# Half of x's turns by VectorE in 32x32 blocks through DRAM, and one product with every engine in written order

## The chip, the cores and the metric

The kernel runs on one core of a Trainium2 chip. A core has a matrix engine (TensorE, PE in the profile), an engine for elementwise work and reductions (VectorE, DVE), an engine for activations, scaled copies and casts (ScalarE, ACT), a general engine (GpSimd, POOL) and an engine that here only starts loads and stores (SyncE, SP). Each takes its instructions in order, and they meet through semaphores. Loads and stores are started from SP's or POOL's queue and carried by 16 DMA engines. SBUF is the on-chip memory with 128 partitions; PSUM holds TensorE's results.

The metric is device time in microseconds (us), median of three runs. Before the change it is 787.09 us (786.91 to 787.52).

## The reference

One layer on x of 512 tokens by 2048 columns, in float32: sliding-window attention with grouped heads, then a gated embedding, then a norm.

```python
hn = rmsnorm(x, norm_g)
y = swa_mixer(hn, ...)              # projections, attention, then (out * silu(gate)) @ w_out
x = x + y
emb = p @ ple_proj
g = sigmoid(rmsnorm(x, ple_norm) @ ple_gate)
x = x + emb * g
return rmsnorm(x, final_g)
```

Two products with 2048x2048 weights follow one another: the output projection (`w_out`) and the gate (`ple_gate`). The second needs the sum x + y with its columns on the partitions, that is transposed ("turned"), and scaled by `ple_norm`. The change is in how, and when, that turning is done.

## The kernel before

A float32 product is made of three matmuls on operands split in two parts: high part by high part, high by low and low by high (`mm3`, the lines that the profile shows as L126 to L128; of 512 columns each). High parts come from a ScalarE cast (`bhi` for weights, `fh...` for the other operand), low parts from a VectorE subtraction of the cast from the original (`blo`, `fl...`).

**Blocks.** Each of the two big products is computed with seven block products in place of eight; one of the seven is itself done the same way with smaller blocks (the `small` names). The six big ones are taken in the order 1, 7, 6, 5, 3, 4. A product is two units (jj = 0, 1) of four steps (m = 0 to 3). A step is one piece of weights (128x1024, 512 KB) and 12 matmuls; after it may come half of a small product, with a piece of its own and 6 matmuls. The product that the change is about is the last of the output projection, p = 4: units (4,0) and (4,1), followed by the first product of the gate, units (1,0) and (1,1).

**One step in written order** (`unit`, L997): fetch the piece (`B.get`); the 12 matmuls; `some_later`, which takes a share of a list of additions to x that earlier products left; `todo`, the step's own chores; `between`, which prepares an operand of a small product and multiplies half a small product. Fetching piece i also issues the cast and the subtraction (the "split", L760 and L761) of piece i + 2. Three buffers hold the casts, so the cast of piece i + 2 waits until TensorE is done with piece i - 1.

**x.** It lies in SBUF as four column groups of 512 (j = 0 to 3), each with four token blocks of 128 (t). A result of a product is added to a block of it by VectorE (`add_to_x`, L1054 and L1056). When a block's last addition is made, ScalarE squares it and sums the squares along the row (`squares`, L1024), in the very next call.

**Turns.** `turn(kp, th)` (L1028) takes two column chunks of 128 (2kp and 2kp + 1) of a half of the tokens (th: blocks 2th and 2th + 1): four 128x128 transposes by TensorE into one PSUM bank (L1038), then two scaled copies of 128x256 by ScalarE into `hT` (L1041). There are 16 such calls, 64 transposes. Twelve are spread over the eight steps of p = 4, those of columns 1024 to 2047 (kp 4 to 7) first; four (kp 0 to 3, second half of the tokens) follow in the four steps of the gate's unit (1,0). `ple_forms.steps(1)` makes the first gate operand, in four parts, from the first half of the tokens of columns 1024 to 2047.

**Who orders the work.** TensorE and SP run in written order throughout. VectorE, ScalarE and GpSimd are in written order in the attention part and from the gate's second product on. In the output projection and in the gate's first product, a planner orders these three, by its own costs: it takes what it holds to be ready, and so moves instructions ahead of earlier-written ones. The load of `final_g` (`fg`, 1 MB on the SP queue) is issued after product 3.

Of the kernel before, what the change touches and what calls it, by code (L numbers as in the profile page):

```python
# [11 lines left out]
F32 = mybir.dt.float32  # L12
# [6 lines left out]
D = 2048  # L19
S = 512  # L20
P = 128
# [34 lines left out]
def trunk_kernel(ctx: ExitStack, tc: tile.TileContext, a: dict):  # L56
    nc = tc.nc
# [12 lines left out]
    pn = const.tile([P, KC], F32, name="pn")  # L70
# [8 lines left out]
    def quarter(name):  # L79
        return whole.tile([P, 4, S], F32, tag="quarter", name=name)  # L80
# [5 lines left out]
    WE = 1024  # L86
# [71 lines left out]
    def run(gen):  # L158
        for _ in gen:
            pass  # L160
# [38 lines left out]
    for k in range(KC):  # L199
# [7 lines left out]
        both = start_pool.tile([P, 2 * 768], F32R, tag="w0s", name=f"w0s{k}")  # L207
# [46 lines left out]
        else:  # L254
            high()
            if k == 1:
                src = xw[:, w_at[512] : w_at[512] + 256]
# [9 lines left out]
        f, e = k == 0, k == KC - 1  # L267
# [18 lines left out]
        for part in "hl" if f else "lh":  # L286
            for t in range(NB):
                c = slice(t * P, (t + 1) * P)
# [6 lines left out]
        if 3 <= k < 3 + NB:  # L295
            t = k - 3
# [18 lines left out]
    def evac_q(c, ps, to=None):  # L315
# [11 lines left out]
        def split(low):  # L327
# [15 lines left out]
            engines={getattr(mybir.EngineType, v) for v in ("PE", "SP", "DVE", "Activation", "Pool")}  # L343
# [57 lines left out]
    for b in range(exact, BUCKETS):  # L401
        d = np.nonzero(bk == b)[0]
        if len(d):
            lo, n = P - 1 + int(d.min()), len(d)
# [301 lines left out]
    for nm, p in SUMS:  # L706
        for q in (6, 5) if (nm, p) == ("ple_gate", 5) else (p,):
            sum_small(nm, q)
        for jj in range(2):
            for m in range(4):  # L710
                t = summed[nm, p, jj, m] = tc.dram_tile([P, WE], F32, name=f"{nm}_{p}_{jj}_{m}")
# [194 lines left out]
    blocks = TWOS * UNITS  # L906
# [83 lines left out]
    later = []  # L990
# [37 lines left out]
    def turn(kp, th, tag):  # L1028
# [10 lines left out]
        for n in range(2):  # L1039
            k = 2 * kp + n  # L1040
            nc.scalar.mul(hT[g][:, k % 4, th * 256 : th * 256 + 256], tp[:, n * 256 : n * 256 + 256], pn[:, k : k + 1])  # L1041

    ple_forms = Forms(swapped, "g")
    ple_first = ple_forms.steps(1)

# [261 lines left out]
    x_at = {(1, 0, 3): 2, (1, 1, 1): 1, (7, 0, 0): 3}  # L1307
    waiting = {(7, 0): (1, 0), (6, 0): (1, 1)}
    held = {}
    for n, p in enumerate(ORDER_OUT):  # L1310
        nxt = out_forms.steps(ORDER_OUT[n + 1]) if n < 5 else iter(())
        for jj in range(2):
            later.extend(held.pop(waiting.get((p, jj)), ()))
            calls = iter(range(4))

            def between(m, ps):
                if (p, jj, m) in EMBED_AT:
                    embedding.slot()
                q = small_steps.get((p, jj, m))
                if q is not None:  # L1320
                    small_out.prepare(q)
                for q in SMALL["w_out"].get((p, jj), {}).get(m, ()):
                    small_out.product(q)

            def todo():
                step = next(calls)
                part = x_at.get((p, jj, step))
                if part is not None:
                    load_x(part, nc.sync)
                part = embed_steps.get((p, jj, step))  # L1330
                if part is not None:
                    embedding.prepare(part)
                next(nxt, None)
                if p == 4:

                    for _ in range({0: 1, 1: 2, 2: 2, 3: 2, 5: 1, 6: 2, 7: 2}.get(4 * jj + step, 0)):
                        turn(*turns.pop(0), "o")
                    if jj:
                        next(ple_first, None)

            ps = unit(p, jj, at_out, out_forms, todo, between)
            posts = [partial_of(add_y, p, jj, tb, ps[tb]) for tb in range(2)]
            if p == 1:
                held[p, jj] = posts
            else:
                later.extend(posts)
        run(nxt)
        if p == 3:
            fg = late.tile([P, D], F32, tag="fg", name="fg")
            nc.sync.dma_start(fg, a["final_g"].partition_broadcast(P))  # L1350
        if p == 3:
            turns = [(kp, th) for kp0, th in ((4, 1), (4, 0), (0, 0)) for kp in range(kp0, kp0 + 4)]
    run(ple_first)
    assert not turns


# [141 lines left out]
    for n, p in enumerate(ORDER_PLE[:-1]):  # L1498
        if n == 1:

            ctx.enter_context(
                tc.manual_schedule(
                    engines={getattr(mybir.EngineType, v) for v in ("PE", "SP", "DVE", "Activation", "Pool")}
                )
            )
        nxt = ple_forms.steps(ORDER_PLE[n + 1])
        for jj in range(2):
            calls = iter(range(4))

            def todo():  # L1510
                step = next(calls)
                k = early.get((p, jj, step))
                if (p, jj, step) in embed_loads:
                    load_embeds(*embed_loads[p, jj, step])
                while small_due:
                    small_due.pop(0)()
                if (p, jj, step) == (5, 0, 2):
                    assert len(moves) == 4
                    while moves:
                        moves.pop(0)()  # L1520
                if (p, jj, step) == (5, 0, 3):
                    for square in moved.pop(0):
                        square()
                if turns:
                    turn(*turns.pop(0), "t")
                    if not turns:
                        nc.vector.tensor_reduce(ss2, ssq2, axis=AX.X, op=ALU.add)
                        run(power_of_mean(rstd2, ss2, "r2"))
                        nc.scalar.activation(ss2[:, :1], ss2[:, :1], AF.Sigmoid)
                    return  # L1530
                next(nxt, None)
                if p == 1:
                    next(nxt, None)
                if k is not None:
                    split_last(k)
                if (p, jj, step) in opens:
                    open_bank(*opens[p, jj, step])

            def between(m, ps):
                if (p, m) == (7, 3):  # L1540
                    gate(p, jj, ps, None)
                q = ple_steps.get((p, jj, m))
                if q is not None:
                    small_ple.prepare(q)
                for q in SMALL["ple_gate"].get((p, jj), {}).get(m, ()):
                    small_ple.product(q)
                if (p, jj, m) == (6, 1, 1):
                    later.append(partial_of(gate_later, "sum", 0, None, embeds_for(1, 0)))

            ps = unit(p, jj, at_ple, ple_forms, todo, between)  # L1550
            last_two, held_e = (p, jj) == (3, 1), {}
            if not (p == 7 or last_two):
                later.insert(0, partial_of(gate_later, p, jj, ps, held_e))
            for of, which in EMBEDS.get((p, jj), ()):
                e = embeds_for(of, which)
                held_e.update(e)
                if of == 1:
                    later.insert(1, partial_of(gate_later, "sum", which, None, dict(e)))
                    held_e.clear()
            if p == 5:  # L1560
                while moved:
                    later.extend(moved.pop(0))
        run(nxt)
# [171 lines left out]
```

## Time and profile before

| | |
|---|---|
| time, median of 3 runs | 787.09 us (786.91 to 787.52) |
| the profiled execution's own time | 787.18 us |
| its span, first to last instruction | 785.5 us |
| mean granted TensorE clock | 0.996 |
| busy: TensorE / VectorE / ScalarE / GpSimd | 775.9 / 612.1 / 528.9 / 149.7 us |
| product p = 4 of the output projection | 587.9 to 624.8 us of the span |
| the gate's unit (1,0) | 624.8 to 637.6 us |

The span is what the profiler saw between the first and the last instruction; the execution's own time holds 1.7 us more around it. Busy times are not additive: the engines work side by side. In a row of the timeline the columns are start, duration, engine, line, operation, output from inputs, shapes and count, and in brackets the idle time of that engine just before, with what ended it. Names of tiles are those of the program without their numbers.

### The profile page before, as it was taken

The numbers are of one execution on the slowest core, as the hardware profiler recorded it, in microseconds if no ns is written. First come the engines' busy times: TensorE is split into PE (matmuls) and PEld (weight loads), VectorE is DVE, ScalarE is ACT, GpSimd is POOL, SyncE is SP. The second block draws the span as 40 slices with busy tenths as digits, with TensorE's granted clock in tenths as the row PEclk, the third lists the DMA queues.
The fourth block names the chain that finished last, engine by engine and source line by source line (L and its number), as shares of the span: only waits on it lengthen the run. The fifth ranks groups of instructions, "written<-read, shape, count | busy, mean of one in ns | idle before, by whom it ended". The sixth has DMA issues, their size and how long they took to land.

```text
span 785.5 us, 11181 instructions
## 1 busy us (share of the span) xinstructions
PE 775.9 (99%) x3700; PEld 648.8 (83%) x3700; DVE 612.1 (78%) x1057; ACT 528.9 (67%) x1121; POOL 149.7 (19%) x273
## 2 busy tenths in 40 slices
PE   9999999999999999999999999999999999999995
PEld 7888888888888888888888888888888888888885
DVE  4547697877877688877878899976897958998996
ACT  6743586766767676766666655678778976667874
POOL 0201423122222314132322200001000002221111
PEclk9999999999999999999999999999999999999998
DMA  9988989999999989999997489868698179999956
GB/s 341 297 210 295 190 251 311 309 287 262 277 265 266 273 235 297 252 302 251 294 252 207 141 318 324 281 204 292 238 374 297 58 298 280 276 280 310 301 116 214
DMA packets 50393, 206.72 MB, mean 263 GB/s; under 512 B 7504, under 2 KB 8528, under 8 KB 44576
## 3 DMA queue, kind: packets, MB, share of 16 engines
q1 hardware_dynamic: 39152, 154.58, 54.9%
q0 software_dynamic: 11184, 51.44, 32.3%
q8 instruction: 29, 0.48, 0.3%
q14 instruction: 28, 0.23, 0.1%
HBM read 192.31 MB, written 75.55 MB: 341 GB/s over the span
## 4 chain that ended last, share of the span: by engine, by line
PE 97%; issue 1%; DMA 0%; DVE 0%; POOL 0%; POOLq 0%; ACT 0%; DVEq 0%; SPq 0%
PE gps L126 7%; PE gps L127 7%; PE gps L128 7%; PE qps L126 7%; PE qps L128 7%; PE qps L127 7%; PE o L127 6%; PE o L128 6%; PE o L126 6%; PE g L128 5%; PE g L127 5%; PE g L126 5%; PE s L485 2%; PE vps L290 2%; PE o L603 2%; PE pt L551 2%
## 5 line engine op out<-in xcount | busy, mean ns | idle before, releaser
L761 DVE TENSOR_TENSOR blo<-braw,bhi 128x1024 fp32r<-128x1024 f32 x100 | 121.9, 1222 | 30.7 <-ACT bhi L760 29.8
L760 ACT CAST bhi<-braw 128x1024 fp32r<-128x1024 f32 x100 | 105.0, 1050 | 39.1 <-PE o L128 15.1
L126 PE MATMUL gps<-xh,whi 128*128 128x512 f32 x256 | 100.0, 390 | 0.0
L127 PE MATMUL gps<-xl,whi 128*128 128x512 f32 x256 | 100.0, 390 | 0.0
L128 PE MATMUL gps<-xh,wlo 128*128 128x512 f32 x256 | 99.8, 390 | 0.0
L126 PE MATMUL qps<-xh,whi 128*128 128x512 f32 x224 | 87.8, 392 | 0.0
L128 PE MATMUL qps<-xh,wlo 128*128 128x512 f32 x224 | 87.5, 390 | 0.0
L127 PE MATMUL qps<-xl,whi 128*128 128x512 f32 x224 | 87.4, 390 | 0.0
L575 POOL TENSOR_SCALAR_AFFINE_SELECT own<-r 64x512 fp32r<-64x512 f32 (+1 forms) x48 | 32.4, 675 | 238.9 <-DVE r L565 235.7
L110 DVE TENSOR_TENSOR wlo<-wraw,whi 128x1024 fp32r<-128x1024 f32 x60 | 73.5, 1227 | 3.4 <-ACT whi L109 3.3
L127 PE MATMUL o<-blo,fho 128*128 128x512 f32 x192 | 74.8, 390 | 0.0
L126 PE MATMUL o<-bhi,fho 128*128 128x512 f32 x192 | 74.8, 390 | 0.0
L128 PE MATMUL o<-bhi,flo 128*128 128x512 f32 x192 | 74.8, 389 | 0.0
L109 ACT CAST whi<-wraw 128x1024 fp32r<-128x1024 f32 x60 | 62.3, 1040 | 5.2 <-issue 4.1
L126 PE MATMUL g<-bhi,fhg 128*128 128x512 f32 x160 | 62.7, 392 | 0.0
L128 PE MATMUL g<-bhi,flg 128*128 128x512 f32 x160 | 62.3, 389 | 0.0
L127 PE MATMUL g<-blo,fhg 128*128 128x512 f32 x160 | 62.3, 389 | 0.0
L128 PEld LDWEIGHTS gps<-xh,wlo 128*128 128x128 f32 x256 | 48.1, 188 | 10.3
L126 PEld LDWEIGHTS gps<-xh,whi 128*128 128x128 f32 x256 | 48.1, 188 | 9.2
L529 ACT ACTIVATE t<-t,sm 128x129 f32<-128x129 f32 (+1 forms) x128 | 49.6, 389 | 8.7 <-DVE sm L525 7.4
L127 PEld LDWEIGHTS gps<-xl,whi 128*128 128x128 f32 x256 | 48.1, 188 | 8.9
L564 ACT CAST r<-pt 128x256 fp32r<-128x256 f32 x56 | 20.8, 372 | 49.9 <-PE pt L551 49.4
(291 smaller groups left out, 1813.2 us busy)
## 6 DMA issues: line engine op xcount, KB each, us to landing
wraw<-in_w_gate_in SPq DMA_DIRECT2D x32, 512.0 KB, 7.7
w_out<-in_w_out POOLq DMA_DIRECT2D x32, 512.0 KB, 9.0
braw<-w_out SPq DMA_DIRECT2D x32, 512.0 KB, 5.4
wraw<-in_w_q SPq DMA_DIRECT2D x28, 512.0 KB, 6.5
braw<-in_w_out SPq DMA_DIRECT2D x22, 512.0 KB, 4.8
braw<-in_ple_gate SPq DMA_DIRECT2D x22, 512.0 KB, 5.8
xw<-in_first SPq DMA_DIRECT2D x14, 640.5 KB, 7.0
w_out<-in_w_out SPq DMA_DIRECT2D x16, 512.0 KB, 10.8
```

The lines of the kernel that those rows point to most:

```text
L109: nc.scalar.copy(hi, raw)
L110: nc.vector.tensor_sub(lo, raw, hi.bitcast(F32))
L126: nc.tensor.matmul(ps, sh, mh, start=first, stop=False, skip_group_check=more)
L127: nc.tensor.matmul(ps, sh, ml, start=False, stop=False, skip_group_check=more)
L128: nc.tensor.matmul(ps, sl, mh, start=False, stop=last, skip_group_check=more)
L290: nc.tensor.matmul(v_ps[t], h[:, c], part_of(high_at, 256, 512), start=f, stop=e, skip_group_check=True)
L485: nc.tensor.matmul(s_ps[:, u, : 2 * n], st, of_keys[:, first * 2 * QB : (first * QB + n) * 2], start=True, stop=True)
L529: nc.scalar.activation(su, su, AF.Exp, bias=sm[:, u : u + 1], accum_out=sm[:, 2 + u : 3 + u])
L564: nc.scalar.copy(rh, src)
L575: nc.gpsimd.affine_select(out=flat(own), in_=flat(r).bitcast(F32), pattern=[[0, 8], [sign, HB]], compare_op=ALU.is_ge, fill=0.0, base=-HB ...
L760: nc.scalar.copy(hi[:, :n], raw)
L761: nc.vector.tensor_sub(lo[:, :n], raw, hi[:, :n].bitcast(F32))
```

## The change

- **Half of the turns leave TensorE.** Columns 1024 to 2047 (j = 2 and 3), both halves of the tokens, are turned in three stages. `turn_blocks`: two VectorE transposes of 128x512, each of which turns every 32x32 block in its place, into a tile of 128x1024, and a 512 KB write of it to DRAM from POOL's queue. `gather_blocks`: four loads of 128 KB from POOL's queue, which bring the blocks of one column chunk together on 32 partitions each, in rows of 1 KB. `scale_turned`: four ScalarE copies of 128x256, scaled by `ple_norm`, from the gathered tile into `hT`. Each stage is there four times (j = 2, 3; th = 0, 1). The tiles written to DRAM come from two buffers in turn, so the third `turn_blocks` waits for the first write to have landed and the fourth for the second.
- **The stages are spread by a table**, `turns_at`: block turns in the four steps of (4,0), gathers from (4,0,2) to (4,1,1), scalings in (4,1,1), (4,1,2), (1,0,1) and (1,0,3).
- **The turns that are left** on TensorE: kp 0 to 3, first half of the tokens, two in each of the last two steps of (4,1); the four of the second half stay where they were. The parts of the first gate operand follow each of those four turns.
- **Product p = 4 is in written order on all engines**, no longer the planner's.
- **Two smaller things.** The two additions that product (3,1) leaves are taken together, at the head of the list, so that both are made in step (4,0,0). The load of `fg` moves from the end of product 3 to step (4,1,1).

```diff
--- before.py
+++ after.py
@@ -1040,6 +1040,48 @@
             k = 2 * kp + n
             nc.scalar.mul(hT[g][:, k % 4, th * 256 : th * 256 + 256], tp[:, n * 256 : n * 256 + 256], pn[:, k : k + 1])
 
+    SQ = P // 4
+    apart, gathered = {}, {}
+
+    def turn_blocks(j, th):
+
+        t = late.tile([P, WE], F32, tag="e", name=f"blocks{j}_{th}", bufs=2)
+        to = t.rearrange("p (a k t q) -> p t k a q", a=4, k=4, t=2)
+        for tb in range(2):
+            assert not missing[j, 2 * th + tb]
+            src = x1[j][:, 2 * th + tb, :].rearrange("p (k a q) -> p k a q", k=4, a=4)
+            nc.vector.transpose(to[:, tb], src)
+        apart[j, th] = tc.dram_tile([P, WE], F32, name=f"apart{j}_{th}")
+        nc.gpsimd.dma_start(apart[j, th], t)
+
+    def gather_blocks(j, th):
+
+        src = apart[j, th].rearrange("(b i) (a x) -> a i b x", b=4, a=4)
+        to = gathered[j, th] = (s7 if th else s1)[:, j % 2].rearrange("p n c -> p (n c)")
+        for quad in range(4):
+            nc.gpsimd.dma_start(to[SQ * quad : SQ * quad + SQ].rearrange("p (b x) -> p b x", b=4), src[quad])
+
+    def scale_turned(j, th):
+
+        if j not in hT:
+            hT[j] = swapped[(j + 2) % 4] = quarter(f"hT{j}")
+        src = gathered[j, th].rearrange("p (b k t q) -> p k b t q", b=4, k=4, t=2)
+        for n in range(4):
+            to = hT[j][:, n, th * 256 : th * 256 + 256].rearrange("p (t b q) -> p b t q", t=2, b=4)
+            nc.scalar.mul(to, src[:, n], pn[:, 4 * j + n : 4 * j + n + 1])
+
+    turns_at = {
+        (4, 0, 0): [(turn_blocks, 2, 0)], (4, 0, 1): [(turn_blocks, 3, 0)],
+        (4, 0, 2): [(gather_blocks, 2, 0), (turn_blocks, 2, 1)], (4, 0, 3): [(gather_blocks, 3, 0), (turn_blocks, 3, 1)],
+        (4, 1, 0): [(gather_blocks, 2, 1)], (4, 1, 1): [(scale_turned, 2, 0), (gather_blocks, 3, 1)],
+        (4, 1, 2): [(scale_turned, 3, 0)],
+        (1, 0, 1): [(scale_turned, 2, 1)], (1, 0, 3): [(scale_turned, 3, 1)],
+    }
+
+    def turns_due(at):
+        for part, j, th in turns_at.get(at, ()):
+            part(j, th)
+
     ple_forms = Forms(swapped, "g")
     ple_first = ple_forms.steps(1)
 
@@ -1307,7 +1349,15 @@
     x_at = {(1, 0, 3): 2, (1, 1, 1): 1, (7, 0, 0): 3}
     waiting = {(7, 0): (1, 0), (6, 0): (1, 1)}
     held = {}
+    fg = None
+    last_out = ExitStack()
     for n, p in enumerate(ORDER_OUT):
+        if p == 4:
+            last_out.enter_context(
+                tc.manual_schedule(
+                    engines={getattr(mybir.EngineType, v) for v in ("PE", "SP", "DVE", "Activation", "Pool")}
+                )
+            )
         nxt = out_forms.steps(ORDER_OUT[n + 1]) if n < 5 else iter(())
         for jj in range(2):
             later.extend(held.pop(waiting.get((p, jj)), ()))
@@ -1323,6 +1373,7 @@
                     small_out.product(q)
 
             def todo():
+                nonlocal fg
                 step = next(calls)
                 part = x_at.get((p, jj, step))
                 if part is not None:
@@ -1332,25 +1383,28 @@
                     embedding.prepare(part)
                 next(nxt, None)
                 if p == 4:
-
-                    for _ in range({0: 1, 1: 2, 2: 2, 3: 2, 5: 1, 6: 2, 7: 2}.get(4 * jj + step, 0)):
+                    turns_due((p, jj, step))
+                if (p, jj, step) == (4, 1, 1):
+                    fg = late.tile([P, D], F32, tag="fg", name="fg")
+                    nc.sync.dma_start(fg, a["final_g"].partition_broadcast(P))
+                if (p, jj) == (4, 1):
+                    for _ in range(2 if step >= 2 else 0):
                         turn(*turns.pop(0), "o")
-                    if jj:
                         next(ple_first, None)
 
             ps = unit(p, jj, at_out, out_forms, todo, between)
             posts = [partial_of(add_y, p, jj, tb, ps[tb]) for tb in range(2)]
             if p == 1:
                 held[p, jj] = posts
+            elif (p, jj) == (3, 1):
+                later.insert(0, lambda both=posts: [post() for post in both])
             else:
                 later.extend(posts)
         run(nxt)
         if p == 3:
-            fg = late.tile([P, D], F32, tag="fg", name="fg")
-            nc.sync.dma_start(fg, a["final_g"].partition_broadcast(P))
-        if p == 3:
-            turns = [(kp, th) for kp0, th in ((4, 1), (4, 0), (0, 0)) for kp in range(kp0, kp0 + 4)]
+            turns = [(kp, 0) for kp in range(4)]
     run(ple_first)
+    last_out.close()
     assert not turns
 
 
@@ -1521,6 +1575,8 @@
                 if (p, jj, step) == (5, 0, 3):
                     for square in moved.pop(0):
                         square()
+                if p == 1:
+                    turns_due((p, jj, step))
                 if turns:
                     turn(*turns.pop(0), "t")
                     if not turns:
```

## The prediction

> **What bounds the kernel now.** I read the page's busy line and the shares of the chain that ended last, then the chain itself around the change, then the timeline of three engines there.
>
> ```profile
> span 785.5 us, 11181 instructions
> PE 775.9 (99%) x3700; PEld 648.8 (83%) x3700; DVE 612.1 (78%) x1057; ACT 528.9 (67%) x1121; POOL 149.7 (19%) x273
> PE 97%; issue 1%; DMA 0%; DVE 0%; POOL 0%; POOLq 0%; ACT 0%; DVEq 0%; SPq 0%
> ```
>
> TensorE sets the end: whatever is taken off it is won, and whatever makes it wait is lost one for one. The profiled execution took 787.18 us, span and 1.7 us around it, against a median of 787.09, so sums on the span carry over less 0.1.
>
> The chain in order of time, from p = 4 into the gate:
>
> ```profile
> 590.80 0.44 PE tp L1038 x4
> 595.37 0.87 PE tp L1038 x8
> 600.37 0.87 PE tp L1038 x8
> 605.35 0.88 PE tp L1038 x8
> 613.26 0.39 PE o L127
> 615.95 0.44 PE tp L1038 x4
> ```
>
> A turn (four transposes) costs TensorE 0.44 us; all lie on the chain. The one other entry, at 613.26, is a matmul whose low part came late; p = 4 has no other stall. The busy times by stretch, the time before p = 4, then (4,0), (4,1) and about (1,0):
>
> ```profile
> core 0: us, PE busy (x) PEld busy (x) DVE busy (x) ACT busy (x) POOL busy (x), PEclk, DMA share, GB/s
> 566.00:587.90 21.90, 21.90 (x98) 18.14 (x97) 19.82 (x24) 16.16 (x22) 0.00 (x0) 1.00 0.96 370
> 587.90:607.50 19.60, 19.60 (x102) 16.45 (x101) 14.76 (x17) 16.21 (x32) 0.00 (x0) 1.00 0.83 305
> 607.50:624.80 17.30, 17.30 (x88) 14.21 (x86) 15.69 (x18) 15.99 (x31) 0.00 (x0) 1.00 0.15 54
> 624.80:641.00 16.20, 16.20 (x82) 13.43 (x80) 8.86 (x12) 13.72 (x27) 1.05 (x1) 1.00 0.63 231
> ```
>
> In p = 4 VectorE and ScalarE have some 10 to 25% to spare, and the planner fits their work to that. GpSimd is idle and the DMA engines nearly so in (4,1).
>
> **What is removed.** Eight turns leave p = 4 (12 become 4): 8 x 0.44 = 3.5 us off TensorE. The 16 ScalarE copies that go with them are replaced by 16 of the same size.
>
> **Units for the walk.** TensorE, then ScalarE, then VectorE, in the timeline of before:
>
> ```profile
> 592.47 0.40 PE L126 MATMUL o<-bhi,fho 128*128 128x512 f32 x1
> ...
> 595.21 1.03 PE L1038 MATMUL tp<-ident,x1s 128*128 128x128 f32 x8
> ...
> 610.15 0.39 PE L126 MATMUL smallo<-bhi,small_aho 128*128 128x512 f32 x1
> ...
> 612.87 0.39 PE L126 MATMUL o<-bhi,fho 128*128 128x512 f32 x1
> 613.15 0.50 PE L127 MATMUL o<-blo,fho 128*128 128x512 f32 x1
> 613.49 0.39 PE L128 MATMUL o<-bhi,flo 128*128 128x512 f32 x1
> ```
>
> ```profile
> 590.88 1.05 ACT L760 CAST bhi<-braw 128x1024 fp32r<-128x1024 f32 x1 [0.17 <-ACT s L1024]
> 595.45 1.05 ACT L760 CAST bhi<-braw 128x1024 fp32r<-128x1024 f32 x1 [0.90 <-ACT s L1024]
> 596.40 1.56 ACT L1041 ACTIVATE hT<-tp,pn 128x256 f32<-128x256 f32 x4
> 602.80 1.06 ACT L760 CAST bhi<-braw 128x1024 fp32r<-128x1024 f32 x1
> 603.74 0.65 ACT L1024 ACTIVATE s<-x1s 128x512 f32<-128x512 f32 x1
> 604.36 0.64 ACT L865 ACTIVATE fhg<-hT 128x512 fp32r<-128x512 f32 x1
> ```
>
> ```profile
> 588.13 1.23 DVE L761 TENSOR_TENSOR blo<-braw,bhi 128x1024 fp32r<-128x1024 f32 x1
> 589.28 0.68 DVE L1054 TENSOR_TENSOR x1s<-o,x1s 128x512 f32<-128x512 f32 x1
> 589.88 1.21 DVE L761 TENSOR_TENSOR blo<-braw,bhi 128x1024 fp32r<-128x1024 f32 x1
> 591.96 1.23 DVE L761 TENSOR_TENSOR blo<-braw,bhi 128x1024 fp32r<-128x1024 f32 x1 [0.27 <-ACT bhi L760]
> 610.74 1.23 DVE L858 TENSOR_TENSOR hT<-hT 128x1024 f32<-128x1024 f32 x1
> 611.88 2.35 DVE L761 TENSOR_TENSOR blo<-braw,bhi 128x1024 fp32r<-128x1024 f32 x2
> ```
>
> A step takes TensorE 2.72 us (592.47 to 595.21), half a small product 1.36 (two from 610.15 to 612.87). A cast can start 0.24 after TensorE has passed to the next piece (595.21, 595.45) and frees ScalarE 0.95 later (596.40). The subtraction starts 1.08 after its cast (590.88, 591.96), and VectorE is free 1.14 later (two in 2.35). An addition takes VectorE 0.60 (589.28 to 589.88), a square ScalarE 0.63 with its read-out (603.74 to 604.36). Four scaled copies took 1.56, of which 0.1 is a tail that overlaps the next (1.05 against 0.95 for a cast): 0.37 each. A form of an operand takes ScalarE 0.52 and VectorE 0.60, as other operations of 512 elements.
>
> So a split of piece i + 2, asked for when piece i starts, is done 0.24 + 1.08 + 1.14 + 0.1 = 2.56 us later. TensorE wants it after pieces i and i + 1, its low part 0.23 after that: 4.08 + 0.23 where a step and a small half lie between (1.75 us to spare), 2.72 + 0.23 where two small halves do (0.39). The stall at 613 stands just behind such a pair: pitches of 0.28 and 0.34 us where 0.227 (2.72/12) is usual, 0.16 in all.
>
> **What is added, bounded.** The block transposes occur in no row before. Below: 0.55 us, 512 elements at the pace that the 1024-element subtraction adds over a 512-element operation (1.22 - 0.68). Above: 1.22, as if it went over its data twice. I take 0.62, nearest to the 512-element rows: eight are 5.0 us of VectorE. [...]
>
> The writes and gathers ride on an idle POOL queue:
>
> ```profile
> 560.68 0.53 POOL L1245 DMA_DIRECT2D embeds<-made  x1 [3.80 <-ACT made L1256]
> embeds<-made POOLq DMA_DIRECT2D x8, 512.0 KB, 4.3
> DMA to landing us min/median/max: 2.9/5.3/11.3
> 628.88 1.05 POOL L1366 TENSOR_TENSOR rstd<-ms_r,power 128x4 f32<-128x4 f32 x1 [67.67 <-DVE ms_r L1364]
> ```
>
> A write of the same shape and queue lands in 4.3 us (by the view of the tile, its loads back included, 2.9 to 11.3). The first block write leaves at about 593, so the third block turn, which needs its buffer and whose turn on VectorE comes near 601, finds it landed up to 8 us; at 11.3 it is 3.3 us late, with two subtractions queued behind it. The gathers are 128 KB each; with 0.55 us per issue the first four land near 606, and the first scaling is due near 616: hidden unless they take 15 us. In (4,1) the DMA share is 0.15, so they and the `fg` load, which leaves the busy stretch before, meet little. POOL's own next work is at 628.88, after the last gather (issued by 615). On SP `fg` passes loads that wait for buffers anyway: nothing.
>
> **What written order costs.** Here the change is not free. In written order a step gives ScalarE: cast, then the square of the block that VectorE has just added to; and VectorE: subtraction, then that addition. The square waits for the addition, the addition stands behind the subtraction, the subtraction behind the cast. ScalarE is not free after 0.95 but after 1.08 + 1.14 + 0.60 + 0.1 + 0.63 = 3.55 us, and the next cast is queued behind. The planner could let the square wait its turn: at 602.80 it put a cast ahead of the square that starts at 603.74. I walk through the queues piece by piece:
>
> (4,0): VectorE has 8 subtractions (9.1), 4 additions (2.4), 8 block transposes (5.0) and three operations for the small operands (1.8), which the planner had partly done before 588: 18.3 us, against 4 x 4.08 = 16.3 of TensorE. It also starts 1.3 late, at 589.2, behind its first cast. 18.3 + 1.3 - 16.3 - 1.75 to spare: a stall of 1.5 us.
>
> (4,1), second step: v0 starts near 605.1; VectorE, behind by the above, ends the addition to x at 610.3, the square ends at 611.0, the cast 612.0, the subtraction 613.25; TensorE wants it at 611.2 + 0.23. Stall 1.9; with VectorE on time it would still be 0.4, since two small halves leave only 0.39.
>
> First gate operand: from the second step of (4,1), time 0: cast, subtraction, addition and square end at 3.8; four scalings 5.3; two casts 7.2; the next subtraction, addition and square end near 9.8 (the wait again); four scalings 11.3; the first turn's two copies 12.0, its form 12.6 and low part 13.3. TensorE reaches the gate at 2.72 + 1.36 + 2.72 + 0.88 + 2.72 + 0.88 = 11.3 and wants the low part 0.45 later. Stall 1.7.
>
> (1,0): the third piece's cast stands behind the rest of the forms and a square that waits; in strict order it is 2.7 late, but this product is still the planner's, which may put that cast into ScalarE's gap (0). I take 0.7, nearer to the planner, since before it moved work for the gate's second product far ahead (L858 at 610.74, for a product that starts after (1,1)).
>
> **Sum:** -3.5 + 1.5 + 1.9 + 1.7 + 0.7 - 0.2 (0.16: the stall at 613 is counted in them) = +2.1: 787.1 + 2.1 = **789.2 us**.
>
> **Rivals.** I call 0.2% (1.6 us) what a measurement can tell from no change.
>
> Faster, 783.6 to 785.3: VectorE keeps up with TensorE in (4,0), so that a step's addition is done soon after its square comes up on ScalarE, and the casts behind are not late. It decides if the squares wait less than about 0.8 us, by which a wait of 3.55 exceeds a step's 2.72. For it: TensorE had no stall with VectorE at 19.8 of 21.9 us just before, and both queues are emptier at 588 by what the planner had pulled forward. Then (4,0) costs nothing, the second step 0.4 and the gate's operand up to 1.3: -3.5 + 0 to 1.7. Against: the wait inside a step comes from the order, not from a backlog. Chance 0.28.
>
> No change, 785.5 to 788.7: two of the three stalls come, 1.9 to 3.6 us in place of 5.8. Chance 0.17.
>
> Forecast, 787.5 to 791.5: chance 0.40.
>
> Much slower, 791 to 793, in three ways. ScalarE's third cast in (1,0) stands behind the forms, 2.0 more than the 0.7 above, 791.2; it decides if the planner's part can't go ahead of the written one (0.07). Or block transposes take 1.22 us: eight times 0.6 more on VectorE, of which (4,0) passes on 3.9 by the same walk, 793.1 (0.05). Or a block write lands in over 8 us: up to +3.3, 792.5 (0.03). [...]
>
> That the turns don't leave TensorE is not to be feared: its matmuls are in written order.
>
> **How the numbers follow.** Faster 0.28. Same takes 0.17 and the low quarter of the forecast's 0.40: 0.26. Slower is the rest, 0.46. The range, 784.0 to 792.5, takes in the better part of the faster case and the usual bounds of the slower; the forecast's own is 787.5 to 791.5.
>
> **What would show it.** Right: the row of `tp` has 32 matmuls, not 64; of the two rows of waits between 585 and 690 below, the first grows to 3 us or more, and the second, 1.1 us in all, comes to 2 us for each square of (4,1); the gate's first matmuls wait for `flg`; (1,0) starts near 627, not 624.8. Wrong: (1,0) starts by 622 with no such wait; then the queues had more room than I walked. Block transposes of over 1 us, or VectorE waiting for a write to DRAM, would make it worse than the sum.
>
> ```profile
> PEld o L127 <- DVE blo L761: 0.3, 1, 0.3
> ACT s L1024 <- DVE x1s L1054: 1.1, 2, 0.7
> ```

## The result and the profile after

| | before | after |
|---|---|---|
| time, median of 3 runs | 787.09 us | 794.06 us (793.92 to 794.10) |
| span of the profiled execution | 785.5 us | 792.0 us |

The changed kernel is slower: ratio 1.0087, 95% interval 1.0064 to 1.011. The forecast was 789.2 us with a range to 792.5: the side is right, the size is 4.9 us short.

The page of the changed kernel, span, busy times and the shares of the chain that ended last:

```profile
span 792.0 us, 11157 instructions
PE 777.4 (98%) x3668; PEld 647.2 (82%) x3668; DVE 617.0 (78%) x1065; ACT 528.6 (67%) x1121; POOL 161.3 (20%) x293
PE 93%; DVE 2%; issue 2%; ACT 2%; POOL 0%; POOLq 0%; DVEq 0%; ACTq 0%
```

TensorE has 32 matmuls fewer and yet 1.5 us more busy time; VectorE and ScalarE now hold 2% of the chain each, and issue another 2%. The busy times by stretch, with the columns of the prediction's table, show where:

```profile
587.90:607.50 19.60, 19.21 (x84) 15.21 (x83) 18.56 (x24) 11.72 (x19) 6.36 (x12) 1.00 0.89 266
607.50:624.80 17.30, 14.78 (x66) 11.05 (x64) 11.31 (x12) 10.88 (x21) 4.64 (x9) 1.00 1.03 322
624.80:641.00 16.20, 13.87 (x57) 10.85 (x58) 10.26 (x13) 14.64 (x33) 1.06 (x1) 0.79 0.55 154
641.00:660.00 19.00, 19.00 (x87) 15.54 (x86) 14.24 (x15) 16.75 (x27) 1.81 (x2) 1.00 0.93 332
```

(4,1), the second row, had only the small stall at 613 before; now TensorE idles 2.5 us in it, while VectorE and ScalarE are busy for less time than before (11.3 and 10.9 against 15.7 and 16.0): they wait for each other, VectorE up to 3.3 us for a cast (at 619.54), ScalarE for additions. In the third row, in which the gate starts, the granted clock (the share of full speed that TensorE's clock was given) is 0.79. The waits from 560 to 700 us (engine, line and tile, what it waited for: total, times, longest):

```profile
ACT s L1024 <- DVE x1s L1096: 13.6, 6, 3.3
...
PEld tp L1038 <- ACT hT L1041: 3.0, 2, 2.2
...
PEld smallo L127 <- DVE blo L761: 1.9, 3, 0.7
...
PEld g L126 <- DVE x1s L1096: 1.6, 1, 1.6
...
PEld o L127 <- DVE blo L761: 1.1, 1, 1.1
```

The squares' waits grew from 1.1 to 13.6 us, six of 1.9 to 3.3 us. The waits that the timeline marks on TensorE, in order of time:

```profile
599.95 0.50 PE L127 MATMUL smallo<-blo,small_aho 128*128 128x512 f32 x1 [0.32 <-DVE blo L761]
608.70 0.50 PE L127 MATMUL smallo<-blo,small_aho 128*128 128x512 f32 x1 [0.26 <-DVE blo L761]
612.13 0.49 PE L126 MATMUL o<-bhi,fho 128*128 128x512 f32 x1 [0.60 <-ACT bhi L760]
613.39 0.50 PE L127 MATMUL o<-blo,fho 128*128 128x512 f32 x1 [0.76 <-DVE blo L761]
625.63 0.66 PE L1038 MATMUL tp<-ident,x1s 128*128 128x128 f32 x4 [1.73 <-ACT hT L1041]
626.87 1.12 PE L1038 MATMUL tp<-ident,x1s 128*128 128x128 f32 x4 [0.58 <-ACT hT L1041]
630.19 0.80 PE L126 MATMUL g<-bhi,fhg 128*128 128x512 f32 x1 [0.92 <-DVE x1s L1096]
```

The third turn of (4,1) waits for ScalarE's copies of the first, and the fourth for the second's: they take the same PSUM banks. ScalarE in that place has a square that waits, four scalings behind it, then the copies:

```profile
622.54 0.63 ACT L1024 ACTIVATE s<-x1s 128x512 f32<-128x512 f32 x1 [2.08 <-DVE x1s L1096]
623.07 0.18 ACT L1024 ACTIVATION_READ_ACCUMULATOR s<-x1s 128x1 f32 x1
623.17 1.69 ACT L1071 ACTIVATE hT<-s,pn 128x256 f32<-128x256 f32 x4
624.76 0.82 ACT L1041 ACTIVATE hT<-tp,pn 128x256 f32<-128x256 f32 x2
625.48 0.62 ACT L865 ACTIVATE fhg<-hT 128x512 fp32r<-128x512 f32 x1
626.00 0.82 ACT L1041 ACTIVATE hT<-tp,pn 128x256 f32<-128x256 f32 x2
```

The last matmul of p = 4, and the gate's first, with the granted clock of that stretch (columns as above):

```profile
623.51 0.39 PE L128 MATMUL o<-bhi,flo 128*128 128x512 f32 x1
...
627.64 0.78 PE L126 MATMUL g<-bhi,fhg 128*128 128x512 f32 x1
...
632.91 0.63 PE L126 MATMUL g<-bhi,fhg 128*128 128x512 f32 x1
633.34 0.52 PE L127 MATMUL g<-blo,fhg 128*128 128x512 f32 x1
```

```profile
627.50:632.00 4.50, 3.58 (x10) 2.44 (x9) 3.85 (x7) 4.50 (x11) 0.36 (x1) 0.50 0.52 148
```

The gate starts at 627.64 in place of 624.79, and its first 12 matmuls take until 633.93, 6.29 us; before they took 2.82 (624.79 to 627.61). The clock fell at 626.76, within the turns, and came back at 633.59. At a clock of 0.50 a matmul's pitch, from start to start, is 0.43 us (632.91 to 633.34) in place of 0.227. From 634 on there is no stall that lasts. The block transposes, and the DMA from 588 to 625 us (KB each, median us to landing):

```profile
L1053 DVE STREAM_TRANSPOSE blocks<-x1s x8: 667/684/706, 591.6 to 606.2; 128x512 f32<-128x512 f32 x8
braw<-in_ple_gate SPq DMA_DIRECT2D x5, 512.0 KB, 17.4
apart<-blocks POOLq DMA_DIRECT2D x4, 512.0 KB, 7.3
s<-apart POOLq DMA_DIRECT2D x16, 128.0 KB, 7.9
```

In the kernel before, the gate's weights landed in 5.2 us there:

```profile
braw<-in_ple_gate SPq DMA_DIRECT2D x6, 512.0 KB, 5.2
```

### The profile page after: what moved, and what is told of

It is laid out like the page before. It is cut to its first block, busy times and chain, and to the rows that moved or that the text cites. A ratio compares the mean times of both kernels' runs of the same rounds, so it can differ in the third digit from the quotient of the medians.

```text
span 792.0 us, 11157 instructions
## 1 busy us (share of the span) xinstructions
PE 777.4 (98%) x3668; PEld 647.2 (82%) x3668; DVE 617.0 (78%) x1065; ACT 528.6 (67%) x1121; POOL 161.3 (20%) x293
## 4 chain that ended last, share of the span: by engine, by line
PE 93%; DVE 2%; issue 2%; ACT 2%; POOL 0%; POOLq 0%; DVEq 0%; ACTq 0%
PE gps L127 7%; PE gps L126 7%; PE gps L128 7%; PE qps L126 7%; PE qps L128 7%; PE qps L127 7%; PE g L126 5%; PE g L127 5%; PE g L128 5%; PE o L127 5%; PE o L128 5%; PE o L126 5%; PE s L485 2%; PE vps L290 2%; PE o L603 2%
## 5 line engine op out<-in xcount | busy, mean ns | idle before, releaser
L760 ACT CAST bhi<-braw 128x1024 fp32r<-128x1024 f32 x100 | 104.1, 1049 | 37.8 <-PE o L128 13.6
L128 PEld LDWEIGHTS gps<-xh,wlo 128*128 128x128 f32 x256 | 48.1, 188 | 10.2
L565 DVE TENSOR_TENSOR r<-pt,r 128x256 fp32r<-128x256 f32 x56 | 23.7, 424 | 38.8 <-ACT r L564 38.0
```

The costliest lines, as they stand in the source:

```text
L128: nc.tensor.matmul(ps, sl, mh, start=False, stop=last, skip_group_check=more)
L565: nc.vector.tensor_sub(rl, src, rh.bitcast(F32))
L760: nc.scalar.copy(hi[:, :n], raw)
```

## The experiments

Each ran beside the kernel before on the same chip (787.0 to 787.5 us). Those that start from the changed kernel compare with its 794.06 us.

**Which part of the change costs.** First the changed kernel without its written order:

```diff
-        if p == 4:
-            last_out.enter_context(tc.manual_schedule(...all engines...))
```

> The changed kernel, but with product p = 4 left to the planner as before; the turns by way of DRAM stay. Theory (the loss is written order: squares on ScalarE wait for additions on VectorE that stand behind subtractions): the planner lets the squares stand aside, 3.5 us of turns leave TensorE and little is lost, 783.5 to 787 us. Rival (the new work itself is the loss: block transposes overload VectorE, the trip through DRAM and the scalings overload ScalarE): 790 us or more.

Measured: 792.24 us (790.84 to 792.71). The planner doesn't save the change. The time is the rival's, but the rows show the order and not the load: it put the scalings ahead on ScalarE, before the gather had landed; a cast and a square stood behind them, and TensorE waited 2.67 us for that cast:

```profile
595.18 1.31 ACT L1071 ACTIVATE hT<-s,pn 128x256 f32<-128x256 f32 x3 [5.47 <-DMA s<-apart]
...
597.48 0.50 PE L126 MATMUL smallo<-bhi,small_aho 128*128 128x512 f32 x1 [2.67 <-ACT bhi L760]
```

Then the kernel before with the written order alone, and the same with two edits that e3 and e4 below introduce:

> The kernel before, with its twelve TensorE turns, but product p = 4 in written order on all engines. Theory: the same waits of squares for additions, with no gain against them; walked through the queues with the durations of the rows of before, TensorE reaches the gate's unit (1,1) 6 us later: 789 to 794 us. Rival: written order costs under 1 us, 786.5 to 788 us.

> The kernel before (all turns by TensorE) with the written order in p = 4, which alone gave 799.8 us, and in it each square one step after its addition and (4,0)'s second addition at (4,1,1). Theory: the square that waits in ScalarE's queue and the bank that the late addition holds are what the written order costs, as in the changed kernel, where these two edits took 5.4 of its 7.0 us back: 787 to 790 us. Rival: the written order costs by something else when TensorE keeps all turns (its turns' copies on ScalarE, 12 turns of two copies): 793 us or more.

```diff
+    def squares_due():            # called at each step of p = 4
+        while ready: ready.pop(0)()
+        ready.extend(owed); owed.clear()
...
-            squares(t, j)
+            (owed.append if late_squares else call)(partial_of(squares, t, j))
...
+                if (p, jj, step) == (4, 1, 1):
+                    some_later(1)
```

Measured: 799.79 us (ratio 1.0162, 1.0145 to 1.0179) and 788.37 us (1.0015, 1.0006 to 1.0025). Written order costs 12.6 us with all turns on TensorE, twice what was expected and above its range; a square written one step after its addition, and one addition written two steps earlier, take 11.4 of them back. So it isn't the order as such but two things in what is written; the two were not run apart here.

**The same two in the changed kernel**, one after the other:

> The changed kernel, with each square of p = 4 written one step after its addition; nothing else. Theory: ScalarE no longer waits for VectorE; by the same walk TensorE stalls 1.7 us in p = 4 and (1,0) against 3.5 us won, 784 to 786 us, and the TensorE clock does not drop. Rival (load of VectorE and DMA): 791 to 794 us.

> As the run with later squares, and the second addition that (4,0) leaves is made in step (4,1,1) in place of (4,1,3), so that its PSUM bank is free for the gate's first product. Theory: 1.0 us better than the run with later squares alone, 783 to 785 us. Rival (that bank costs nothing once the squares are out of the way): the same as that run.

Measured: 789.96 us (788.76 to 790.94), then 788.70 us (787.81 to 790.04): 4.1 us for the squares and 1.3 more for the addition, both times above the ranges expected. No square waits for its addition any longer, and the 2.31 us that TensorE waits for the bank in e3 are gone in e4. In e4 a cast now waited for its weights:

```profile
616.94 1.05 ACT L760 CAST bhi<-braw 128x1024 fp32r<-128x1024 f32 x1 [2.51 <-DMA braw<-in_ple_gate]
```

**The transfers.** Four kernels. In e5 the block transposes are left out and x is written to DRAM as it is, so the blocks aren't turned; e7 (from e4) replaces the four gathers of 1 KB rows by one straight load of 512 KB, so the blocks aren't brought to place; e6 is e4 with the load of `fg` back behind product 3; e8 (from e6) scatters on the write in place of the gather and computes all.

```diff
-            nc.vector.transpose(to[:, tb], src)                         # e5
-        nc.gpsimd.dma_start(apart[j, th], t)
+        nc.gpsimd.dma_start(apart[j, th]..., x1[j][:, 2 * th : 2 * th + 2, :])
...
-            nc.gpsimd.dma_start(to[SQ * quad ...], src[quad])           # e7, four times
+        nc.gpsimd.dma_start(to, apart[j, th])
...
-                if (p, jj, step) == (4, 1, 1):                          # e6, e9
-                    nc.sync.dma_start(fg, ...)
+        if p == 3:
+            nc.sync.dma_start(fg, ...)
```

> The changed kernel with VectorE's eight block transposes left out: the blocks of x go to DRAM as they lie, so the columns are not turned inside the 32x32 blocks; that part of the computation is left out, all else is as it was. Theory (waits of squares for additions set the loss): VectorE has 5 us less to do in (4,0), and by the walk 1.3 us come back, 792 to 793.5 us. Rival (the block transposes' load on VectorE sets the loss): 790 us or less.

> As the run with later squares and the earlier addition (788.7 us), with each gather's four loads of 1 KB rows onto 32 partitions replaced by one load of the same 512 KB in rows of 4 KB onto 128 partitions, so that the blocks are not brought to their places; that part of the computation is left out. If the shape of the gathers is what holds up the weights, the loads of weights land in under 10 us and the time is 785 to 787 us. If it is the bytes, or the fg load alone, they land in 15 us or more and the time stays at 788 to 789 us.

> As the run with later squares and the earlier addition (788.7 us), with the 1 MB load of fg back where it was before the change, after product 3. Theory (what is left is DMA: a cast waited 2.5 us for its weights, whose loads landed in 17.7 us in place of 5.2, queued behind fg and among the gathers): the wait falls under 1 us and the stalls behind it with it, 785 to 787 us. Rival (ScalarE's load in (4,1) and (1,0) is what is left): 788 to 789 us.

> As the run with fg back, with the 1 KB rows on the other leg of the trip: each block write goes to DRAM as four scattered writes, and each gather is one load of 4 KB rows. All is computed. If 1 KB rows cost as much written as read, the same as the run with fg back within 0.5 us; if reading them onto 32 partitions is the costly part, 0.5 to 1.5 us better; if DRAM takes small writes badly, the block writes land later, VectorE waits for their buffer, and it is 1 us worse or more.

Measured: e5 796.07 us (794.9 to 796.65), 2.0 us slower than with the transposes and outside both expectations. Without them the writes leave sooner (the first at 574.5 in place of 594.1), the weights land in 20.0 us, a cast waits 3.1 us for them, and TensorE waits longer for the turns' copies behind it:

```profile
627.36 2.35 PE L1038 MATMUL tp<-ident,x1s 128*128 128x128 f32 x8 [4.75 <-ACT hT L1041]
```

So this run doesn't price the transposes alone. That they need not cost anything is shown by e13 below, which has all eight and no wait of TensorE.

e7: 790.29 us (790.21 to 791.28), 1.6 us worse than e4. Neither expectation holds: the weights landed sooner (14.4 us), but the scaling waited for the straight load itself, and TensorE behind it:

```profile
ACT hT L1070 <- DMA s<-apart: 4.1, 1, 4.1
```

e6: 785.88 us (785.39 to 787.77; ratio 0.9986, 0.9977 to 0.9995): 2.8 us better than e4, by the place of one 1 MB load, as its theory had it. No cast waits for a load any more. e8: 787.68 us (1.0008, 0.9999 to 1.0016), 1.8 us worse than e6. The weights landed in 8.3 us in place of 13.5, but VectorE waited for a buffer whose scattered write had not landed, and TensorE for a subtraction behind it, as the third case of the expectation had it:

```profile
DVE blocks L1053 <- DMA apart<-blocks: 1.0, 1, 1.0
```

```profile
604.36 0.50 PE L127 MATMUL smallo<-blo,small_aho 128*128 128x512 f32 x1 [0.80 <-DVE blo L761]
```

In the changed kernel itself, the load's place decides nothing:

> The changed kernel with one edit: the load of fg is issued after p = 3's products again, as in the kernel before; squares, the addition of (4,0), turns by VectorE and the written order stay. Theory: in the changed kernel itself no ScalarE cast waited for a transfer, and its loss comes from the waiting squares, the PSUM banks of the turns and of (4,0)'s second addition, and the half clock behind them; so the load's place, worth 2.8 us once these were gone, is worth little here: 792.5 to 794.5 us. Rival: the slow transfers are the main cause in the changed kernel too: 791 or below, by the 2.8 us that it was worth there.

Measured: 793.97 us (793.52 to 794.16); its stalls are those of the changed kernel to 0.1 us. The theory holds: there the casts came late for other reasons, which hid the late weights.

**ScalarE's copies.** In e6 the gate starts 3.4 us ahead of before (621.39 against 624.79), but only 1.4 us arrive at the end (785.88 us against 787.30 beside it). ScalarE was busy without a gap in (1,0), and TensorE waited 0.76 us for one of its forms. The 16 scalings went to GpSimd (e10), or the eight of (1,0) to VectorE (e13):

```diff
-            nc.scalar.mul(to, src[:, n], pn[...])
+            nc.gpsimd.tensor_scalar_mul(to, src[:, n], pn[...])    # e10
+            nc.vector.tensor_scalar_mul(to, src[:, n], pn[...])    # e13, th = 1
```

> The best kernel so far (squares one step later, (4,0)'s second addition at (4,1,1), fg loaded after p = 3's products; 785.88 us) with the 16 scaled copies of the gathered turns on GpSimd, which is idle there, in place of ScalarE. Theory: what is left there is the rest of ScalarE's load in (4,1) and (1,0) (6.4 us of copies), so that 784.5 to 785.5 us come out. Rival: ScalarE is no longer on the path, and GpSimd's copies are slower or stand behind the gathers that it issues: 786 us or more.

> The best kernel so far (785.88 us) with the eight scaled copies of (1,0) on VectorE in place of ScalarE. In the best kernel ScalarE is busy 16.2 of 16.2 us from 624.8 to 641 and VectorE 10.4, and TensorE waits 0.76 us at 640.6 for a form that ScalarE makes late. Theory: what is missing to the 3.5 us taken off TensorE is ScalarE's load there; without 3.4 us of copies that wait goes, and 784.6 to 785.5 us come out. Rival: the copies delay the subtractions on VectorE, or the rest is lost elsewhere: 785.7 us or more.

Measured: e10 793.57 us (793.23 to 795.31), 7.7 us worse than e6, the rival's side: four take GpSimd 5.1 us, where ScalarE takes 1.7, and a subtraction that stands behind the late result on VectorE stops TensorE:

```profile
613.53 5.11 POOL L1071 TENSOR_SCALAR hT<-s,pn 128x256 f32<-128x256 f32 x4
...
631.97 0.50 PE L127 MATMUL g<-blo,fhg 128*128 128x512 f32 x1 [2.28 <-DVE blo L761]
```

e13: 783.74 us (783.60 to 783.86; ratio 0.9958, 0.9945 to 0.997), faster than both kernels clear of noise, and below the range expected. VectorE makes four in 1.1 us; the timeline marks no wait of TensorE from 585 to 700, and the stretch with (1,0) shows it full (columns as above):

```profile
629.44 1.14 DVE L1072 TENSOR_SCALAR hT<-s,pn 128x256 f32<-128x256 f32 x4
```

```profile
624.80:641.00 16.20, 16.20 (x78) 13.38 (x78) 14.71 (x23) 16.17 (x29) 3.70 (x1) 1.00 0.83 290
```

It is 3.3 us faster than the kernel before it ran beside, where 3.5 came off TensorE: all but 0.2 of the gain arrives once nothing else is lost.

**The half clock.** It came with long waits. In the profiled executions up to e11 it came in or behind a wait of TensorE of 1.73 us or more in the changed kernel, e1, e3, e5, e7, e9 and e10, and in e2 twice, behind a wait of 1.96 us and behind two of 1.16 and 0.76 close together; e4 (1.06 and 1.22), e8 (0.80), e11 (0.81) and e6 (0.76) had none. But a long wait does not always bring it: in e10 the 2.28 us shown above, and another 1.92 us at 637.38, left the clock at 1.00 (columns as above):

```profile
628.00:641.00 13.00, 8.80 (x44) 6.80 (x43) 8.95 (x10) 8.13 (x15) 8.92 (x7) 1.00 0.33 95
```

To see whether the idle stretch is the cause, eight matmuls that nobody reads were put into the waits (e12); then the bank's wait was taken away by the earlier addition, alone (e14) and with the eight (e15):

```diff
+                        if step == 3:
+                            filler(6 if len(turns) == 2 else 2)
                         turn(*turns.pop(0), "o")
```

> The changed kernel with eight added matmuls whose result nobody reads: six ahead of the third turn of (4,1) and two ahead of the fourth, where TensorE waits 1.73 and 0.58 us in the changed kernel (6 x 0.227 = 1.36 and 2 x 0.227 = 0.45 us, so they fit into the waits). They hold no answer for any other engine: every wait of the others stays. Theory: the half clock from 627.5 to 634 comes from TensorE having done next to nothing but turns and waits for 3.7 us; with the gap filled the first gate matmuls keep a pitch of 0.227 us instead of 0.43, and the time falls by the 2.4 us that this cost, to 791 to 792.3 us. Rival: the clock falls for another reason (the chip's load, ScalarE, the block transposes), and the time stays at 793.5 us or more.

> The changed kernel with one edit: the second addition of (4,0) at (4,1,1) in place of (4,1,3), so that the gate's second PSUM bank is free when TensorE comes to it; squares as in the changed kernel. Theory: only the 0.92 us at 630.2 go, the turns' waits of 1.7 and 0.6 us stay, and the half clock behind them too: 792.3 to 793.6 us, with a granted clock of about 0.8 from 624.8 to 641. Rival: the earlier addition brings its squares forward into (4,1), where each waits in ScalarE's queue, and the turns' copies come as much later: 794 us or more.

> The kernel of e14 with the eight added matmuls of e12, whose result nobody reads, in TensorE's waits before the third and the fourth turn of (4,1). In e12 the first gate matmuls kept the pitch of 0.227 us, but the wait of 1.97 us for the bank stood behind them, and the half clock came after that one. Theory: with the bank free no idle stretch of over 1.5 us is left, the clock stays at 1.00 through (1,0), and the time is 1.5 to 2.5 us below that of e14, though nothing that TensorE waits for comes sooner. Rival: the drop does not follow from TensorE's idle stretch; it comes with or without the added matmuls, and the two differ by less than 0.7 us.

Measured: e12 794.02 us (791.95 to 794.44), not the 791 to 792.3 of the theory, though one of its five runs lies there. The rows of the profiled execution, the slowest of the five, say why:

```profile
627.93 0.40 PE L128 MATMUL g<-bhi,flg 128*128 128x512 f32 x1
630.30 0.50 PE L126 MATMUL g<-bhi,fhg 128*128 128x512 f32 x1 [1.97 <-DVE x1s L1106]
...
631.56 0.40 PE L128 MATMUL g<-bhi,flg 128*128 128x512 f32 x1
631.79 0.60 PE L126 MATMUL g<-bhi,fhg 128*128 128x512 f32 x1
632.19 0.63 PE L127 MATMUL g<-blo,fhg 128*128 128x512 f32 x1
```

The gate's first three matmuls ran at full pace; then came 1.97 us of waiting for the bank, which nothing had moved, and six matmuls later the half clock. With the bank free, e14 took 793.12 us (791.89 to 794.08) and e15 792.18 us (792.02 to 793.09). From 624.8 to 641, e14 and then e15:

```profile
624.80:641.00 16.20, 14.03 (x65) 11.50 (x66) 10.12 (x13) 15.70 (x35) 1.06 (x1) 0.89 0.62 164
```

```profile
624.80:641.00 16.20, 15.41 (x79) 12.27 (x78) 10.77 (x13) 16.20 (x36) 1.06 (x1) 1.00 0.55 158
```

With the waits filled the clock stays at 1.00, without the added matmuls it doesn't, and the two kernels differ in nothing else: here the idle stretch is the cause, as far as one profiled execution of each can show it. The price was smaller than the theory's 1.5 to 2.5 us: in e14 the half clock ended at 630.3, after four matmuls, and e15 is 0.94 us faster. Their ranges overlap (791.89 to 794.08, 792.02 to 793.09), so it is the clock's row and not the time that decides.

What is taken away does not all come back, either. e15 has neither the bank's wait nor the half clock, and it is done with the gate's first 12 matmuls 3.4 us sooner than the changed kernel (630.53 against 633.93); its span is only 1.8 us shorter (790.2 against 792.0). Some 0.6 us of the rest is lost at 646.80, where TensorE waits for a form that ScalarE makes late.

## Why the prediction was right and wrong

**Right.** Eight turns came off TensorE. A block transpose of 128x512 takes 0.61 us at pitch (two in 1.3), where 0.62 was taken, and not the 1.22 of the slow case. The stalls at the small halves of (4,0) and the first step of (4,1) come to 1.5 us: 0.35 (at 595.25, too short for the list above), 0.58 and 0.53 over the usual pitch. 1.5 were foreseen, but all in (4,0), where 0.9 fell. The one at the second step of (4,1), 1.9 us (1.9 foreseen). The wait was named as it is: the square stands on ScalarE for an addition that stands behind a subtraction, and casts stand behind the square; the runs e3 and e11 show it by taking it away.

**Wrong: "Stall 1.7" ahead of the gate.** It was 3.0 us: 623.51 + 0.23 for the last matmul, 0.88 for two turns, and the gate starts at 627.64; 0.3 of it is the fourth turn itself, which ran at half clock (0.77 in place of 0.44). The step that failed is "TensorE reaches the gate at ... = 11.3". It let the last two turns run when their place in TensorE's order came; but they need the banks of the two turns before, whose copies stood on ScalarE behind the late square and four scalings. The forecast followed the copies only to the form they feed, not to the bank they free. Its signs say the same: no matmul of the gate waited for `flg`, whose first low part was done at 626.82, 0.8 us before the gate started, and the row of `o` waiting for `blo` came to 1.1 us, not 3 (3.0 with the row of `smallo`). Three of its sums are slightly off, and change nothing here: 13.3 less 11.3 and 0.45 is a stall of 1.6; stalls of 1.9 to 3.6 us would give 785.5 to 787.2, not 788.7; and 0.17 with a quarter of 0.40 is 0.27.

**Wrong: the 0.7 in (1,0).** The third cast did go ahead of the square, as the planner was trusted to do, and cost nothing. In its place stood a bank again: the second addition of (4,0), written only in (4,1,3), held the gate's second result for 0.92 us. In e14, which writes it earlier, that wait is gone; its time is 0.94 us lower, with a range that overlaps that of the changed kernel.

**Missing: the clock.** The forecast had no term for it. The gate's first 12 matmuls took 3.47 us more than before; 0.92 is the bank, some 2.5 is the half clock. So -3.5 + 1.5 + 1.9 + 3.0 is 2.9, about the 2.85 us by which the gate starts late, and 3.47 make 6.3 of the span's 6.5 us. Of the missing 4.9 us, 1.3 are at the turns (0.3 of them clock), 0.2 at the bank and 2.5 of clock; 0.2 are the credit that it gave for the old stall at 613 and that the sum of the new ones does not need; the last 0.7, between this stretch and the median, weren't followed. These are shares of the trace; taking the bank's wait and the half clock away is worth less, as e15 shows.

**"So they and the `fg` load ... meet little", "on SP ... nothing."** For the changed kernel's time this held (e9), for the wrong reason: the DMA share of (4,1) rose from 0.15 to 1.03 and the gate's weights landed in 17.4 us in place of 5.2. The prediction read 0.15 as room, when the change itself was about to fill it with writes, gathers and 1 MB. The lateness was covered by the other stalls; with those gone it cost 2.8 us (e4 to e6). That `fg` passes loads on SP which wait for buffers anyway did not keep it from slowing them: the weights landed in 17.7 us with it (e4) and in 13.5 without (e6).

**The rivals.** "VectorE keeps up" was wrong for this kernel, since its squares wait by order and not by backlog; but e13, with 783.74, stands where that rival stood, with later squares, an earlier addition, `fg` moved back and half of the scalings on VectorE. Of the three ways to 791 to 793 none came about: third cast, slow transposes, late block writes (7.3 us to landing, and VectorE waited for none). The time came there by a fourth.

## What to carry to other kernels

In written order, don't write an operation directly behind the one it needs when that one stands behind a chain on another engine: one step later cost nothing here and was worth 4.1 us by itself (e3), and 11.4 together with one earlier addition (e11). Follow each late instruction not only to what it feeds but to the buffer or PSUM bank it frees, and where TensorE stalls for some 2 us, reckon with half clock behind it: here it came with most waits of 1.73 us or more, and not with the 2.28 and 1.92 us of e10. A DMA share read from the profile before says nothing of the room left after the change (in (4,1) 0.15 became 1.03); add up what the change sends there, and load what nobody needs yet in another stretch.

## What the runs showed of the hardware

**The clock fell quickly, and for steps of 3.4 us.** In the changed kernel TensorE had only two turns and waits between 623.74 and 627.64, and the granted clock fell to 0.50 at 626.76, 3.0 us into that stretch. In e12 it fell at 631.89, 1.6 us behind a wait of 1.97 us, with three matmuls shortly before it; in e10 a wait of 2.28 us left it at 1.00. In every profiled execution that shows the half clock between 585 and 660 us, it lasted 3.4 us or a multiple: 3.4 in e1, e2 (both times), e3, e10, e12 and e14, 6.8 in the changed kernel, e7 and e9, 10.2 in e5. The two falls of e2, at 619.54 and 636.65, lie 17.1 us apart, five times 3.4. So the moment of a wait may count beside its length; no run varies that alone. In the changed kernel a turn of 0.66 us at 625.63 stands 1.1 us ahead of the fall and did not keep the clock up.

**The same scaled copy on three engines.** Four of 128x256 in float32 from SBUF, strided, took 1.7 us on ScalarE, 1.14 on VectorE and 5.11 on GpSimd (twelve in 13.65). The idle engine was the wrong place for it here.

**Gathers in 1 KB rows and their neighbours.** 128 KB took 7.9 us to land in a stretch where 512 KB loads of weights took 17.4 us, 14.2 without the `fg` load (e9). It counted here beside the bytes how they were moved: with the same bytes, read in 4 KB rows and written in 1 KB rows, the weights landed in 8.3 us (e8) in place of 13.5 (e6), and with straight loads both ways and `fg` in 14.4 us (e7) in place of 17.7 (e4). Each figure is one execution, and when the transfers leave shifts with the rest.
